# Gated linear recurrences in a hybrid block: chunk states replaced by scores of 128 and 256 tokens

## The chip, the cores and the metric

The kernel runs on one core of a Trainium2 chip. The metric is the device time of the program in microseconds (us). Engines are named as the profile names them: PE is TensorE (matmuls; PEld its weight loads), DVE is VectorE, ACT is ScalarE, POOL is GpSimd, SP is SyncE, whose queue issues most DMAs.

## The reference

The block normalises `x` (512 tokens of 2048 features), multiplies it by a wide input matrix, runs two token mixers in parallel, merges them with gates, projects and normalises. The change touches mixer A only, a gated linear recurrence with 8 heads of 128 features. The reference computes it in chunks of 64 tokens with a state between them:

```python
def step(state, inp):
    q_c, k_c, g_c, v_c = inp
    cum = jnp.cumsum(g_c, axis=1)
    inter = jnp.einsum('bthk,bhkv->bthv', q_c * jnp.exp(cum), state)
    diff = cum[:, :, None] - cum[:, None, :]
    decay = jnp.exp(jnp.where(causal[None, :, :, None, None], diff, -jnp.inf))
    scores = jnp.einsum('bthk,bshk,btshk->bhts', q_c, k_c, decay)
    intra = jnp.einsum('bhts,bshv->bthv', scores, v_c)
    last = cum[:, -1]
    new_state = (jnp.exp(last)[..., None] * state
                 + jnp.einsum('bshk,bshv->bhkv', k_c * jnp.exp(last[:, None] - cum), v_c))
    return new_state, inter + intra
```

Written without chunks, the output for token t is the sum over all s up to t of (q at t, times k at s, times the product of the forget gates f between them, summed over the 128 features) times v at s. `f` lies between 0 and 1, `k` is 1 - f. The output then goes through an RMS norm per head and a SiLU gate.

## The kernel before

**The order of the work.** The kernel is one long list of jobs, most of them projections: matmuls of the input matrix with the tokens, each as three float32r products of a high and a low half (`mm3`, lines 74 to 77). Side work is written as Python generators in lanes (line 180). After every few matmuls of a job `pump` (line 195) lets each lane take one step, up to the next `yield`. So the engines' queues hold a projection's matmuls, a step of each lane, the next matmuls, and so on, in the order in which the program issues them. `prep` (line 157) splits the next block of weights into halves, the high one on ACT (line 71), the low one on DVE (line 72), ahead of the matmuls that read them. The recurrences' lane comes first in a pump, ahead of the lane `top`, which selects keys for mixer B on DVE (lines 625 to 642). That lane takes iterations as far as a credit goes, and `R.load`, which the recurrences set before a yield, is the part of the credit that they claim for their own DVE work.

**One pair of heads.** `hgrn_gen(p)` (line 736) computes two heads (c is 0 or 1), and there are four pairs, in the order 3, 2, 0, 1. `q` and `k` are 128 features by 512 tokens for each head, plain float32, in one tile hqk, and all products of this generator use `mm` (line 79) on float32 operands.

- Levels 0 to 7 (lines 816 to 843) build the scores inside blocks of 128 tokens. At level l the tokens fall into halves of m = 2^(l-1); the products of the k of each earlier half with the q of the later half are the scores between the two. Then `decay(l)` (line 772) multiplies, on DVE, the q of the later halves by the total forget of the half before them and the k of the earlier halves by that of the half after them (`tot`), and the totals of two neighbouring halves are multiplied. After level 7, q and k carry the decay to the start and the end of their block of 128 tokens.
- The scores land in S (tile hS): 8 blocks of 128 by 128, four for each head. Small levels are gathered in `near` and copied (`nears`, line 812), levels 6 and 7 are copied by `spread_out` (line 804), all on ACT; S is filled with zeros on POOL beforehand (line 822).
- First step after the levels (lines 848 to 854): the k of blocks 0 to 2 are transposed on PE into a bank hkt (line 852) and copied to hkd (line 853).
- Second step (lines 857 to 870): three products per head, hkd with v, into a bank hp give what each block adds to the state (line 863); ACT copies the first, DVE forms the states of the second and third from the one before (line 867) in hst.
- Third step (lines 871 to 884): for each head seven products of 128 columns into a bank ho: v with the four blocks of S (line 878), and the states with the q of blocks 1 to 3 (line 880). ACT copies the result and its square (lines 881, 882).
- The rest is the norm (sums over features by a product with ones, into hz), the gate, and the split into halves hy that four DMAs write to DRAM (line 912). The tiles hz* and hy* take the places of hkd, hst, hq and hS (lines 886, 887, 909).

Of the kernel before, what the change touches and what calls it, by code (L numbers as in the profile page):

```python
# [26 lines left out]
F32 = mybir.dt.float32  # L27
FR = mybir.dt.float32r
AF = mybir.ActivationFunctionType
OP = mybir.AluOpType  # L30
# [4 lines left out]
T, D = 512, 2048  # L35
# [15 lines left out]
def hybrid_block(ctx, tc, x, w_in, w_uq, w_qidx, w_ukv, w_pa, w_pb, w_out, rel_bias, final_norm_w,  # L51
                 x_t, w_first, w_norm, w_cols, c_ident, c_levels, c_buckets, c_flip, out):
    nc = tc.nc
    V, A, G, PE, SP = nc.vector, nc.scalar, nc.gpsimd, nc.tensor, nc.sync
# [12 lines left out]
    def bank(name):  # L67
        return sdp.tile([128, 512], F32, name=name, tag="sd")
# [10 lines left out]
    def mm(ps, l, r, first, last):  # L79
        PE.matmul(ps, l, r, start=first, stop=last, skip_group_check=True)  # L80
# [35 lines left out]
    R = SimpleNamespace(load=0.0)  # L116
# [74 lines left out]
    def do_soon():  # L191
        while soon:
            soon.popleft()()
# [451 lines left out]
    def place(p, shape, dtype, name, tag):  # L645
        if p == 1 or tag not in ("hf", "hq"):
            return R.h.tile(shape, dtype, name=name, tag=tag)
        return R.i.tile(shape, dtype, name=name, tag=f"{tag}{p or 3}")
# [87 lines left out]
    def hgrn_gen(p):  # L736
        f, q = (hg[p, n] for n in "fq")
        gate = R.h.tile([128, 2, T], F32, name="hg")
        SP.dma_start(gate, gate_d[2 * p:2 * p + 2].rearrange("f p t -> p f t"))
        S = R.h.tile([128, 8, 128], F32, name="hS")  # L740
        near = R.h.tile([128, 8, 32], F32, name="hnear")
        G.memset(near, 0.0)
        qk = R.h.tile([128, 2, 2, T], F32, name="hqk")
# [3 lines left out]
        q0, tot = (a.rearrange("p c t -> p (c t)") for a in (q, f))  # L747
        q, k = qk[:, 0], qk[:, 1]
        qf, kf = (a.rearrange("p c t -> p (c t)") for a in (q, k))
# [4 lines left out]
        def scores(l, ps, qf=qf, kf=kf):  # L754

            m = 1 << l >> 1
            w = max(32, m)
            for n in range(8):
                for h in range(0, 128, w if l < 6 else 2 * w):
                    s = n * 128 + h  # L760
                    if l == 0:
                        o, r = ps[h:h + 32, n * 32:n * 32 + 32], q0[:, s:s + 32]
                    elif l < 6:
                        o = ps[h:h + 32, n * 16:n * 16 + 16]
                        r = qf[:, s:s + 32].rearrange("p (b a t) -> p a b t", a=2, t=m)[:, 1]
                    else:
                        g = h + m * (n % 2)
                        o = ps[g:g + m, n // 2 * m:n // 2 * m + m]
                        r = qf[:, s + m:s + 2 * m]
                    mm(o, kf[:, s:s + w], r, True, True)  # L770

        def decay(l):


            m = 1 << (l - 1)
            nb = 1024 // (2 * m)
            x = bass.AP(tensor=qf.tensor, offset=qf.offset + m, ap=[qf.ap[0], [1024 - m, 2], [2 * m, nb], [1, m]])
            tv = tot.rearrange("p (n a) -> p a n", a=2)
            V.tensor_tensor(x, x, tv[:, :, :, None].to_broadcast([128, 2, nb, m]), op=OP.mult)
            nt = R.h.tile([128, nb], F32, name=f"tot{l}", tag=f"tot{l % 2}")  # L780
            V.tensor_tensor(nt, tv[:, 0, :], tv[:, 1, :], op=OP.mult)
            return nt

        def take(l, ps):
            if l == 0:
                V.copy_predicated(near, R.levels[:, 0:1, :].to_broadcast([128, 8, 32]),
                                  ps[:, 0:256].rearrange("p (n t) -> p n t", n=8))
                return
            m = 1 << (l - 1)
            b = 16 // m  # L790
            mask = R.levels[:, l:l + 1, :].rearrange("p n (b a t) -> p n a b t", a=2, t=m)[:, :, 1]
            V.copy_predicated(near.rearrange("p n (b a t) -> p n a b t", a=2, t=m)[:, :, 1],
                              mask.to_broadcast([128, 8, b, m]),
                              ps[:, 0:128].rearrange("p (n b t) -> p n b t", n=8, t=m))

        def keep(l):

            m = 1 << (l - 1)
            nb = 1024 // (2 * m)
            x = bass.AP(tensor=qf.tensor, offset=qf.offset + m, ap=[qf.ap[0], [1024 - m, 2], [2 * m, nb], [1, m]])  # L800
            o = bass.AP(tensor=q0.tensor, offset=q0.offset + m, ap=[q0.ap[0], [-m, 2], [2 * m, nb], [1, m]])
            A.activation(o, x, AF.Copy)

        def spread_out(l, ps):
            m = 1 << (l - 1)
            for h in range(0, 128, 2 * m):
                for e in range(2):
                    g = h + m * e
                    A.activation(S[h:h + m, e::2, h + m:h + 2 * m],
                                 ps[g:g + m, 0:4 * m].rearrange("p (n t) -> p n t", n=4), AF.Copy)  # L810

        def nears(hs):
            for h in hs:
                A.activation(S[h:h + 32, :, h:h + 32], near[h:h + 32], AF.Copy)

        for l in range(1, 8):
            R.load = (0, 2.9, 1.6, 2.2, 1.5, 2.1, 1.4, 1.4)[l]
            if l % 2 == 0:
                do_soon()
                tot = decay(l)  # L820
                if l == 4:
                    G.memset(S, 0.0)
                if l == 6:
                    nears((0, 32))
                yield
                continue
            ps = bank("hl")
            at = 128 if l < 7 else 256
            if l == 1:
                scores(0, ps[:, 128:384])  # L830
            else:
                scores(l - 1, ps[:, at:at + 128], q0, q0)
            scores(l, ps)
            tot = decay(l)
            if l < 7:
                take(l - 1, ps[:, at:])
                take(l, ps)
                soon.append(lambda l=l: keep(l + 1))
            else:
                spread_out(6, ps[:, at:])  # L840
                spread_out(7, ps)
                nears((64, 96))
            yield

        R.load = 0.0
        if p == 1:
            yield
        kd = R.h.tile([128, 2, 3, 128], F32, name="hkd")
        for c in range(2):
            pt = bank("hkt")  # L850
            for j in range(3):
                PE.transpose(pt[:, j * 128:(j + 1) * 128], k[:, c, j * 128:(j + 1) * 128], R.ident)
            A.activation(kd[:, c], pt[:, :384].rearrange("p (j t) -> p j t", j=3), AF.Copy)
        yield
        while (p, "v") not in hg:
            yield
        R.load = 1.4
        v = hg[p, "v"]
        st = R.h.tile([128, 2, 3, 128], F32, name="hst")
        for c in range(2):  # L860
            pp = bank("hp")
            for j in range(3):
                mm(pp[:, j * 128:(j + 1) * 128], kd[:, c, j, :], v[:, j, c * 128:(c + 1) * 128],
                   j == 0, True)
            A.activation(st[:, c, 0, :], pp[:, 0:128], AF.Copy)
            for j in (1, 2):
                V.scalar_tensor_tensor(st[:, c, j, :], st[:, c, j - 1, :],
                                       tot[:, c * 4 + j:c * 4 + j + 1],
                                       pp[:, j * 128:(j + 1) * 128], op0=OP.mult, op1=OP.add)
        yield  # L870
        sq = k
        zs = []
        o = place(p, [128, 2, T], F32, "ho", "hf")
        for c in range(2):
            po = bank("ho")
            for j in range(4):
                sl = slice(j * 128, (j + 1) * 128)
                mm(po[:, sl], v[:, j, c * 128:(c + 1) * 128], S[:, 4 * c + j, :], j == 0, j == 0)
                if j:
                    mm(po[:, sl], st[:, c, j - 1, :], q[:, c, sl], False, True)  # L880
            A.activation(o[:, c], po, AF.Copy, scale=128 ** -0.5)
            A.activation(sq[:, c], po, AF.Square, scale=128 ** -0.5)
        R.load = 0.0
        yield
        for c in range(2):
            zs.append((place(p, [128, T], FR, "hzh", ("hkd", "hst")[c]),
                       place(p, [128, T], FR, "hzl", ("hq", "hS")[c])))
            split(*zs[c], sq[:, c])
        R.load = 1.4
        yield  # L890
# [2 lines left out]
        for c in range(2):  # L893
            ps = bank("hz")
# [10 lines left out]
        V.tensor_tensor(sq, sq, o, op=OP.mult)  # L905
        yield
        R.load = 1.3
        for c in range(2):
            y = [place(p, [128, T], FR, f"hy{i}", (("hkd", "hst"), ("hq", "hS"))[i][c]) for i in range(2)]
            split(*y, sq[:, c])  # L910
            for i in range(2):
                late[1].append(lambda y=y[i], i=i, h=2 * p + c: SP.dma_start(ya_d[i, h], y.bitcast(F32)))
# [713 lines left out]
```

## Time and profile before

| | |
|---|---|
| median of 3 runs | 1341.34 us (1340.42 to 1341.58) |
| the profiled execution | 1340.78 us |
| its span, first to last instruction | 1339.0 us |
| PE, DVE, ACT busy | 1328.2, 1067.2, 667.4 us |
| DVE combinations of states, line 867 | 16, each about 347 ns |
| ACT copies of transposes, line 853 | 8, each about 492 ns |
| ACT copies of 512 columns out of ho, line 881 | 8, each about 598 ns |

The profile is of one execution. Its page gives each engine's busy time and the chain of work that ended last. The views by tile list the instructions that write or read a tile (out<-in), with the least, median and largest duration in ns, their first and last start, and their shapes (partitions x elements). The chain in order of time and the timeline have a start in us, a length in us and an instruction (x4 means four merged into one line). A matmul's duration runs from its start to its modelled end, so neighbouring matmuls overlap; in the chain each has only the stretch that was its own. The view of waits says which engine and line waited for which, in total, how often, and at most. A row of the view of stretches has the stretch, its length, the busy time and count of PE, PEld, DVE, ACT and POOL, the granted clock of TensorE, the share of the DMA engines and GB/s.

### The profile page before, as it was taken

What the parts mean: (1) busy time and instruction counts of PE and PEld (TensorE: products, weight loads), DVE (VectorE), ACT (ScalarE), POOL (GpSimd) and SP (SyncE); (2) the same over time, 40 slices, a digit from 0 to 9 for tenths busy, and PEclk for the clock granted to TensorE, in tenths of its full rate; (3) what the DMA queues carried; (4) which work ended last, traced back from release to release, by engine and by line L of the source; (5) the groups of instructions that cost most, each with busy time, mean ns of one, the idle gap of its engine ahead of it and who ended that gap; (6) DMA issues with size and microseconds to landing.
All of it is one profiled execution on the core that took longest, in us unless ns stands there. A gap on an engine that the chain in (4) does not pass through costs nothing.

```text
span 1339.0 us, 26559 instructions
## 1 busy us (share of the span) xinstructions
PE 1328.2 (99%) x10876; PEld 1236.8 (92%) x10876; DVE 1067.2 (80%) x1705; ACT 667.4 (50%) x1060; POOL 35.7 (3%) x54
## 2 busy tenths in 40 slices
PE   9999999999999999999999999999999999999997
PEld 9988999999999999999999888888888888899996
DVE  7777889998888888886879989775656658899856
ACT  6455555454454444444666464656434423444435
POOL 2000000000000000000000000020001000000000
PEclk9999999999999999999999999999999999999999
DMA  6344545543454444434523525445755556653564
GB/s 242 95 114 113 151 142 158 154 138 104 142 158 143 142 142 142 135 107 164 182 84 103 182 72 159 125 151 176 242 191 191 186 177 218 202 161 124 163 208 164
DMA packets 141290, 205.82 MB, mean 154 GB/s; under 512 B 8672, under 2 KB 82032, under 8 KB 141040
## 3 DMA queue, kind: packets, MB, share of 16 engines
q1 hardware_dynamic: 140592, 203.78, 48.3%
q8 instruction: 85, 1.39, 0.4%
q10 hardware_dynamic: 576, 0.35, 0.1%
q14 instruction: 37, 0.30, 0.1%
HBM read 168.42 MB, written 35.68 MB: 152 GB/s over the span
## 4 chain that ended last, share of the span: by engine, by line
PE 95%; DVE 2%; ACT 1%; DMA 1%; issue 0%; SPq 0%; DVEq 0%; ACTq 0%
PE pp L75 15%; PE pp L77 15%; PE pp L76 15%; PE acc L75 14%; PE acc L77 14%; PE acc L76 14%; PE hl L80 1%; PE ho L80 1%; DMA xt<-in_x_t_dram 1%; PE sc L75 1%; PE sc L76 1%; PE sc L77 1%; PE hp L80 0%; PE po L77 0%; DVE xl L341 0%; PE po L76 0%
## 5 line engine op out<-in xcount | busy, mean ns | idle before, releaser
L150 ACT ACTIVATE bh<-wr 128x768 fp32r<-128x768 f32 x128 | 108.2, 845 | 215.5 <-issue 94.5
L152 ACT ACTIVATE wh<-sv 128x512 fp32r<-128x512 f32 x256 | 152.5, 623 | 84.3 <-DVE sv L145 66.6
L77 PE MATMUL pp<-sh,wl 128*128 128x256 f32 x624 | 172.7, 277 | 0.0
L75 PE MATMUL pp<-sh,wh 128*128 128x256 f32 x624 | 172.7, 277 | 0.0
L76 PE MATMUL pp<-sl,wh 128*128 128x256 f32 x624 | 172.6, 277 | 0.0
L72 DVE TENSOR_TENSOR wl<-wr,wh 128x1024 fp32r<-128x1024 f32 (+1 forms) x104 | 125.5, 1207 | 57.0 <-ACT wh L71 57.0
L154 DVE TENSOR_TENSOR wl<-sv,wh 128x1024 fp32r<-128x1024 f32 x128 | 156.4, 1222 | 5.8
L153 DVE TENSOR_TENSOR bl<-wr,bh 128x768 fp32r<-128x768 f32 x128 | 122.2, 955 | 47.2 <-ACT bh L150 46.9
L71 ACT ACTIVATE wh<-wr 128x1024 fp32r<-128x1024 f32 (+1 forms) x104 | 108.2, 1040 | 94.3 <-PE acc L76 40.6
L75 PE MATMUL acc<-xh,wh 128*128 128x512 f32 x304 | 120.3, 396 | 0.0
L77 PE MATMUL acc<-xh,wl 128*128 128x512 f32 x304 | 118.6, 390 | 0.0
L76 PE MATMUL acc<-xl,wh 128*128 128x512 f32 x304 | 118.5, 390 | 0.0
L76 PEld LDWEIGHTS pp<-sl,wh 128*128 128x128 f32 x624 | 117.3, 188 | 0.0
L77 PEld LDWEIGHTS pp<-sh,wl 128*128 128x128 f32 x624 | 117.3, 188 | 0.0
L75 PEld LDWEIGHTS pp<-sh,wh 128*128 128x128 f32 x624 | 117.3, 188 | 0.0
L75 PE MATMUL pp<-xh,bh 128*128 128x256 f32 x416 | 114.8, 276 | 0.0
L77 PE MATMUL pp<-xh,bl 128*128 128x256 f32 x416 | 114.8, 276 | 0.0
L76 PE MATMUL pp<-xl,bh 128*128 128x256 f32 x416 | 114.8, 276 | 0.0
L75 PE MATMUL acc<-yh,wh 128*128 128x512 f32 x256 | 100.3, 392 | 0.0
L76 PE MATMUL acc<-yl,wh 128*128 128x512 f32 x256 | 99.7, 390 | 0.0
L77 PE MATMUL acc<-yh,wl 128*128 128x512 f32 x256 | 99.7, 389 | 0.0
L145 DVE TENSOR_TENSOR sv<-wr 128x512 f32<-128x512 f32 x128 | 87.8, 686 | 8.2 <-DMA wr<-in_w_in_dram 5.1
(390 smaller groups left out, 3605.2 us busy)
## 6 DMA issues: line engine op xcount, KB each, us to landing
wr<-in_w_in_dram SPq DMA_DIRECT2D x136, 512.0 KB, 3.8
wr<-in_w_out_dram SPq DMA_DIRECT2D x32, 512.0 KB, 3.8
mg<-gate_d SPq DMA_DIRECT2D x48, 256.0 KB, 4.4
gate_d<-c SPq DMA_DIRECT2D x44, 256.0 KB, 4.7
wr<-in_w_in_dram SPq DMA_DIRECT2D x36, 256.0 KB, 3.0
wr<-in_w_pa_dram SPq DMA_DIRECT2D x16, 512.0 KB, 4.6
wr<-in_w_pb_dram SPq DMA_DIRECT2D x16, 512.0 KB, 4.1
wr<-in_w_qidx_dram SPq DMA_DIRECT2D x8, 512.0 KB, 4.0
```

Of the source, the lines that this page charges most:

```text
L71: A.activation(hi, src, AF.Copy)
L72: V.tensor_tensor(lo, src, hi.bitcast(F32), op=OP.subtract)
L75: PE.matmul(ps, lh, rh, start=first, stop=False, skip_group_check=True)
L76: PE.matmul(ps, lh, rl, start=False, stop=False, skip_group_check=True)
L77: PE.matmul(ps, ll, rh, start=False, stop=last, skip_group_check=True)
L80: PE.matmul(ps, l, r, start=first, stop=last, skip_group_check=True)
L145: V.tensor_tensor(sv[:, 0:2, :], b[:, 1:3, :], b[:, 0:1, :].to_broadcast([128, 2, 256]), op=OP.add)
L150: A.activation(bh, b[:, 1:4, :], AF.Copy)
L152: A.activation(vh[:, i:i + 2, :], sv[:, i:i + 2, :], AF.Copy)
L153: V.tensor_tensor(bl, b[:, 1:4, :], bh.bitcast(F32), op=OP.subtract)
L154: V.tensor_tensor(vl, sv, vh.bitcast(F32), op=OP.subtract)
```

## The change

States, transposes and `tot` as a multiplier of states go. In their place come two more levels of scores, between blocks of 128 tokens (level 8: blocks 0 and 1, blocks 2 and 3) and between halves of 256 tokens (level 9: blocks 0 and 1 with blocks 2 and 3), so that S holds the scores of every block with itself and every later block: ten blocks of 128 by 128 for each head in place of four. They lie in such an order that the scores of one block j with blocks j to 3 can be read at a constant step.

- First step: for each head two products of 128 columns, all four into one bank h8, and one copy on ACT into S; then one multiply on DVE over 512 elements (k of block 0 by the total of block 1, q of block 3 by the total of block 2, both heads), in place.
- Second step: for each head two products of 256 columns into a bank h9, and a copy on ACT.
- Third step: for each head four products, the v of block j with the whole row of scores, 512, 384, 256 and 128 columns wide, added up in the bank ho.
- S grows from 8 to 20 blocks, hkd and hst are gone, and the tiles of the norm and of the split take places in hS and hq. Only the four blocks on the diagonal of each head are filled with zeros.

```diff
-        S = R.h.tile([128, 8, 128], F32, name="hS")
+        S = R.h.tile([128, 20, 128], F32, name="hS")
+
+        def blocks(at, dims, s=S):
+            return bass.AP(tensor=s.tensor, offset=s.offset + at * 128, ap=[s.ap[0], *dims])
...
                 if l == 4:
-                    G.memset(S, 0.0)
+                    G.memset(blocks(3, [[1280, 2], [-128, 4], [1, 128]]), 0.0)
...
-        kd = R.h.tile([128, 2, 3, 128], F32, name="hkd")
+        ps = bank("h8")
         for c in range(2):
-            pt = bank("hkt")
-            for j in range(3):
-                PE.transpose(pt[:, j * 128:(j + 1) * 128], k[:, c, j * 128:(j + 1) * 128], R.ident)
-            A.activation(kd[:, c], pt[:, :384].rearrange("p (j t) -> p j t", j=3), AF.Copy)
+            for i in range(2):
+                s = slice(i * 256, i * 256 + 128)
+                mm(ps[:, (2 * c + i) * 128:(2 * c + i + 1) * 128], k[:, c, s],
+                   q[:, c, i * 256 + 128:i * 256 + 256], c == 0 and i == 0, True)
+        A.activation(blocks(5, [[1280, 2], [384, 2], [1, 128]]),
+                     ps.rearrange("p (c i t) -> p c i t", c=2, i=2), AF.Copy)
+        x = bass.AP(tensor=qf.tensor, offset=qf.offset + 384, ap=[qf.ap[0], [640, 2], [512, 2], [1, 128]])
+        tv = bass.AP(tensor=tot.tensor, offset=tot.offset + 2, ap=[tot.ap[0], [-1, 2], [4, 2], [0, 128]])
+        V.tensor_tensor(x, x, tv, op=OP.mult)
+        R.load = 0.7
+        yield
+        for c in range(2):
+            ps = bank("h9")
+            for i in range(2):
+                mm(ps[:, i * 256:i * 256 + 256], k[:, c, i * 128:i * 128 + 128], q[:, c, 256:512], i == 0, True)
+            A.activation(blocks(10 * c + 7, [[-384, 2], [256, 2], [1, 128]]),
+                         ps.rearrange("p (i n t) -> p i n t", i=2, n=2), AF.Copy)
+        R.load = 0.0
         yield
...
-        R.load = 1.4
         v = hg[p, "v"]
-        st = R.h.tile([128, 2, 3, 128], F32, name="hst")
-        for c in range(2):
-            pp = bank("hp")
-            for j in range(3):
-                mm(pp[:, j * 128:(j + 1) * 128], kd[:, c, j, :], v[:, j, c * 128:(c + 1) * 128],
-                   j == 0, True)
-            A.activation(st[:, c, 0, :], pp[:, 0:128], AF.Copy)
-            for j in (1, 2):
-                V.scalar_tensor_tensor(st[:, c, j, :], st[:, c, j - 1, :],
-                                       tot[:, c * 4 + j:c * 4 + j + 1],
-                                       pp[:, j * 128:(j + 1) * 128], op0=OP.mult, op1=OP.add)
-        yield
...
             for j in range(4):
-                sl = slice(j * 128, (j + 1) * 128)
-                mm(po[:, sl], v[:, j, c * 128:(c + 1) * 128], S[:, 4 * c + j, :], j == 0, j == 0)
-                if j:
-                    mm(po[:, sl], st[:, c, j - 1, :], q[:, c, sl], False, True)
+                n = (4, 3, 2, 1)[j]
+                mm(po[:, j * 128:], v[:, j, c * 128:(c + 1) * 128],
+                   blocks(10 * c + 3 - j, [[(256, 256, 896, 128)[j], n], [1, 128]]), j == 0, j == 3)
...
+        z = place(p, [128, 3, T], FR, "hzs", "hS")
+        zs = [(z[:, 0], place(p, [128, T], FR, "hzl", "hq")), (z[:, 1], z[:, 2])]
...
+        ys = place(p, [128, 3, T], FR, "hys", "hS")
```

The left-out lines adapt `spread_out` and `nears` to the new order of the blocks in S, with as many copies of the same sizes, and drop the tiles that z and y had.

More of the change, by code (lines that the diff above doesn't have):

```diff
@@ L808, in spread_out @@
                     g = h + m * e
-                    A.activation(S[h:h + m, e::2, h + m:h + 2 * m],
-                                 ps[g:g + m, 0:4 * m].rearrange("p (n t) -> p n t", n=4), AF.Copy)
+                    o = blocks(3 - e, [[1280, 2], [-256, 2], [1, m]], S[h:h + m, :, h + m:h + 2 * m])
+                    A.activation(o, ps[g:g + m, 0:4 * m].rearrange("p (c i t) -> p c i t", c=2, i=2), AF.Copy)
         def nears(hs):
             for h in hs:
-                A.activation(S[h:h + 32, :, h:h + 32], near[h:h + 32], AF.Copy)
+                o = blocks(3, [[1280, 2], [-128, 4], [1, 32]], S[h:h + 32, :, h:h + 32])
+                A.activation(o, near[h:h + 32].rearrange("p (c j) t -> p c j t", c=2), AF.Copy)
         for l in range(1, 8):
@@ L884, in hgrn_gen @@
         yield
+        z = place(p, [128, 3, T], FR, "hzs", "hS")
+        zs = [(z[:, 0], place(p, [128, T], FR, "hzl", "hq")), (z[:, 1], z[:, 2])]
         for c in range(2):
-            zs.append((place(p, [128, T], FR, "hzh", ("hkd", "hst")[c]),
-                       place(p, [128, T], FR, "hzl", ("hq", "hS")[c])))
             split(*zs[c], sq[:, c])
@@ L907, in hgrn_gen @@
         R.load = 1.3
+        ys = place(p, [128, 3, T], FR, "hys", "hS")
         for c in range(2):
-            y = [place(p, [128, T], FR, f"hy{i}", (("hkd", "hst"), ("hq", "hS"))[i][c]) for i in range(2)]
+            y = [ys[:, c], place(p, [128, T], FR, "hyl", "hq") if c == 0 else ys[:, 2]]
             split(*y, sq[:, c])
```

## The prediction

> **What bounds the kernel now.** I read the page first, then TensorE's waits and the stretches of time, then the matmuls of the part that changes, one tile at a time, with the chain of waits beside them.
>
> ```profile
> span 1339.0 us, 26559 instructions
> ...
> PE 1328.2 (99%) x10876; PEld 1236.8 (92%) x10876; DVE 1067.2 (80%) x1705; ACT 667.4 (50%) x1060; POOL 35.7 (3%) x54
> ...
> PE 95%; DVE 2%; ACT 1%; DMA 1%; issue 0%; SPq 0%; DVEq 0%; ACTq 0%
> ```
>
> TensorE is busy for 99% of the span and holds 95% of the chain that ended last. A busy TensorE need not be at its peak, since a matmul's recorded end is modelled, so I also look at what it waited for, and at the stretch in which the four pairs of recurrences run (from about 690 us to 925 us).
>
> ```profile
> engine line waited for: us in total, times, longest us
> PE acc L310 <- POOL ones_r L306: 1.4, 1, 1.4
> PE hl L80 <- DVE hqk L779: 0.7, 1, 0.7
> PE pf L80 <- POOL fh L336: 0.3, 1, 0.3
> PE pf L80 <- ACT xh L340: 0.3, 1, 0.3
> ```
> ```profile
> 690.00:925.00 235.00, 234.34 (x2969) 204.35 (x2968) 189.61 (x371) 133.19 (x211) 10.01 (x14) 1.00 0.43 131
> ```
>
> In those 235 us TensorE is busy for 234.34 (the first figure after the length), at the full clock (1.00). The one wait there is 0.7 us, for VectorE's decay before the last level. VectorE is busy 189.61 us and ScalarE 133.19 us, so both have room. Between the steps of a pair the projections' matmuls run, and they never starve. Hence the rule for this change: a microsecond of matmul added to these steps is a microsecond of the end, one taken away likewise, and VectorE's or ScalarE's work counts only where TensorE comes to wait for it.
>
> **What the steps cost now.** The rows of the tiles hkt (transposes), hp (chunk states), ho (values) and st (elsewhere, but the one plain float32 matmul that is 512 columns wide):
>
> ```profile
> L852 PE MATMUL hkt<-ident,hqk x24: 271/272/273, 721.0 to 896.7; 128*128 128x128 f32 x24
> ```
> ```profile
> L80 PE MATMUL hp<-hv,hkd x48: 271/275/275, 724.4 to 900.7; 128*128 128x128 f32 x48
> ```
> ```profile
> L80 PE MATMUL ho<-hS,hv x64: 270/275/275, 728.6 to 907.5; 128*128 128x128 f32 x64
> ...
> L80 PE MATMUL ho<-hqk,hst x48: 275/275/275, 729.0 to 907.7; 128*128 128x128 f32 x48
> ```
> ```profile
> L380 PE MATMUL st<-dg,ones_r x2: 590/590/591, 43.1 to 43.5; 128*128 128x512 f32 x2
> ```
>
> Counts first. A pair does 6 products into hp, so 24 over four pairs, and there are 48 records: a plain float32 matmul leaves two records. A transpose leaves one (6 by 4 is 24). The 275 ns are the time from a record's start to its modelled end and overlap with the next record; what a record costs is its share of the chain:
>
> ```profile
> 43.22 0.86 PE st L380 x2
> ...
> 737.77 0.93 PE hz L80 x4
> ```
> ```profile
> 721.17 0.66 PE hkt L852 x6
> 724.56 1.34 PE hp L80 x12
> 728.73 3.12 PE ho L80 x28
> ...
> 899.67 1.34 PE hp L80 x12
> ...
> 904.87 3.12 PE ho L80 x28
> ```
>
> So a record of 128 columns costs 1.34/12 or 3.12/28, 0.111 us each time, transposes too (0.66/6 is 0.110), and one of 512 columns costs 0.86/2, 0.43 us. That is 3.9 times the price for 4 times the columns: TensorE is paced by columns, and there is almost no fixed price per record. The line through the two points is 0.83 ns for a column and 0.005 us for a record, which gives 0.217 us at 256 columns and 0.324 at 384 (estimates between two measured ends).
>
> **The change on TensorE, for one pair.** Removed: the transposes (0.66), the chunk states (1.34) and the old values (3.12), together 5.12 us. Added:
> - Level 8, four products of 128 columns: 8 records by 0.111, 0.89 us.
> - Level 9, four products of 256 columns: 8 records by 0.217, 1.74 us.
> - Values, for each of the two heads one product each of 512, 384, 256 and 128 columns: of each width 4 records, 4 by (0.43 + 0.324 + 0.217 + 0.111), 4.33 us.
>
> The new sum is 6.96 us, 1.84 us more; over four pairs 7.4 us. There are fewer instructions (32 records for 46) but more columns: the two heads had 20 products of 128, 2560 columns, and now have 4096, while the six transposes saved were single records. The fourteen records saved are worth 14 times 0.005 us, which is in the sum already.
>
> These columns are what it costs to carry no state: the old form folds three chunks into states and reads one state for each later chunk; the new one multiplies every chunk's values by the scores of every chunk from there on.
>
> **The change on the other engines.** VectorE loses four combinations of 128 columns per pair (line 867) and gains one multiply of 512 elements, half of a decay. ScalarE loses two copies of 384 and two of 128 columns, and gains three of 512. All stand beside TensorE's work, with the projections' matmuls between the steps as cover (2.8 us from 721.58 to 724.40 in the rows below), and I count them at nothing, except for one wait. The filling of S with zeros covers as many elements as before. The number of yields is the same (three), so no queue is passed, SyncE's and GpSimd's included; the pool is as large as before (S grows by what the two dropped tiles held), and the y tiles go out by the same four DMAs; the zero fill of the next pair has to wait for the last of the four today already, since that one lies in S. The background selection on VectorE is told a load of 0.7 in one step in place of 1.4 in the next, which moves less than one of its iterations.
>
> **The added wait.** Level 9 needs the new multiply, which waits behind all that VectorE has queued, and the multiply waits for level 8, whose operands it overwrites. In its place stood hp, which waited only for ScalarE's copy of the transposes. How late VectorE would be is read from the step as it stands, in the first pair and in the third:
>
> ```profile
> 718.93 1.22 DVE L779 TENSOR_TENSOR hqk<-hqk,tot 128x1024 f32<-128x1024 f32 x1
> ...
> 723.69 1.23 DVE L72 TENSOR_TENSOR wl<-wr,wh 128x1024 fp32r<-128x1024 f32 x1 [1.03 <-ACT wh L71]
> 724.83 0.42 DVE L639 MAX8 m<-M 128x8 f32<-128x256 f32 x1
> ```
> ```profile
> 722.59 1.06 ACT L71 ACTIVATE wh<-wr 128x1024 fp32r<-128x1024 f32 x1
> 723.54 0.87 ACT L853 ACTIVATE hkd<-hkt 128x384 f32<-128x384 f32 x2
> ```
> ```profile
> 721.01 0.82 PE L852 MATMUL hkt<-ident,hqk 128*128 128x128 f32 x6
> 721.58 0.37 PE L75 MATMUL acc<-wh,xh 128*128 128x256 f32 x1
> ...
> 724.40 1.50 PE L80 MATMUL hp<-hv,hkd 128*128 128x128 f32 x12
> ```
> ```profile
> 840.01 1.23 DVE L72 TENSOR_TENSOR wl<-wr,wh 128x1024 fp32r<-128x1024 f32 x1 [1.17 <-ACT wh L71]
> 841.16 0.69 DVE L639 MAX8 m<-M 128x8 f32<-128x512 f32 x1
> ```
> ```profile
> 842.28 1.50 PE L80 MATMUL hp<-hv,hkd 128*128 128x128 f32 x12
> ```
>
> On ScalarE the copy of the transposes (line 853) comes behind the weight split wh, so that split is queued ahead of this step, and VectorE's half of it, wl, stands ahead of the new multiply. In the first pair wl ends at about 724.83 us. The multiply takes half of the decay's 1.22, 0.61 us, and is done at 725.44. TensorE would want level 9 at 724.40 plus 0.23 (level 8 is 0.89 where the transposes took 0.66), at 724.63: a stall of 0.8 us. While it waits, the projections behind it in order wait too, and nothing gives it back. In the third pair wl ends at 841.16, the multiply at 841.8, and level 9 is due at 842.5: room of 0.7 us. I take 0.8 us once. Its ends are nothing (if VectorE gets the multiply ahead of wl) and about 0.9 us in each pair, 3.6 us.
>
> **The sum.** 7.4 and 0.8 make 8.2 us. The profiled execution took 1340.78 us, so 1349.0 us; the median of the runs shown, 1341.34, is 0.56 above that execution.
>
> **Rivals.**
>
> *Wide records are cheap* (the other side: faster). If a record were paced by something other than its columns, by its weight load or its issue, wide rows would win. The place is level 9 and the values. The price: the float32r record of 512 columns (hz above) costs 0.93/4, 0.23 us, and if plain float32 cost no more at that width, with 0.174 and 0.116 at 384 and 256, level 9 would be 0.93 us and the values 2.53; with level 8 that is 4.35 us, 0.77 less than today, 3.1 us less over four pairs, 1337.7 us. It decides from the point where a 512-column record costs under about 0.29 us (there 0.89, level 9 and the values add up to 5.12 again). The row against it is st: 0.43.
>
> The Trainium skill, "TensorE: Matmul & The Clock Gate", section "Back-to-back issue gap", says for sustained streams that a matmul of 128 columns takes about 81 ns and one of 512 about 131. By that ratio of 1.62 a 512-column record would be 0.18 us here, and the kernel some 3.3 us faster (an estimate from that page). This trace disagrees, with its ratio of 3.9.
>
> *No change.* The added columns fill gaps that TensorE has, or the shorter work of VectorE gives time back. The gap in the stretch is 0.7 us in all, and it lies before level 7, ahead of anything that changes. At most 1341 us, and only if the steps' matmuls do not delay what follows, against 234.34 busy of 235.
>
> *More waits.* The multiply is late in all four pairs, or ScalarE's copies of the levels come late for the values: 7.4 and up to 3.6 us, about 1351.8. For it: the first pair is late by its rows. Against it: the third pair has room, and seven levels with the same pattern of decay and product cost one wait of 0.7 us in four pairs.
>
> **How the numbers follow.** 0.82 for the forecast, 0.11 for more waits, 0.04 for no change, 0.03 for cheap wide records. A measurement of this kernel can tell about 0.2%, 2.7 us, from no change; the first two cases are slower by more than that. So faster 0.03, same 0.04, slower 0.93. For the range: without the stall the time is 1348.1, from which I take the 0.7 us wait, should the shift of the steps remove it, and 1.2 us, by which the runs shown differ (1340.42 to 1341.58): 1346.2. The top is more waits, 1351.8, with 0.7 us for the runs: 1352.5.
>
> **What would show it.** Right: hkt and hp are gone; the chain has 8 records of level 8 in about 0.89 us, 8 of level 9 in about 1.74, and 16 of the values in about 4.33 per pair; TensorE's busy time and the span both grow by some 8 us; its waits gain one row of about 0.8 us, for VectorE's new multiply. Wrong: 16 value records in under 3 us (columns are not the price), a TensorE that waits in every pair for the multiply or for a copy, or a stretch from level 1 of the first pair to the end of the last that is not longer than today.

## The result, and the profile after

The changed kernel took 1350.13 us (median of 4 runs, 1349.23 to 1350.79), the kernel before 1340.92 us beside it (4 runs). The ratio is 1.0066, with a 95% interval of 1.0053 to 1.0079: slower by 9.2 us, where 8.2 were forecast; the time lies 1.1 us above the forecast of 1349.0 and inside its range of 1346.2 to 1352.5. A second set of runs of the same kernel gave 1349.34 us against 1341.17, 8.2 us more (ratio 1.0062, 1.0049 to 1.0075). The profiled execution of the changed kernel took 1350.32 us.

The page after, the lines that answer to those of before:

```profile
span 1348.5 us, 26429 instructions
...
PE 1337.3 (99%) x10820; PEld 1238.8 (92%) x10820; DVE 1065.9 (79%) x1693; ACT 668.3 (50%) x1056; POOL 38.5 (3%) x54
...
PE 96%; DVE 2%; ACT 1%; DMA 0%; issue 0%; POOL 0%; SPq 0%; ACTq 0%
```

TensorE is still busy for 99%, and its busy time grew by 9.1 us with 56 fewer records: the span (9.5 us more) follows TensorE, not the count of instructions. Not all of the 9.1 us is the change: the products account for 7.2, as the chain below shows, and about 1.0 is a later start, which the next section takes up. What TensorE waited for, after:

```profile
PE acc L310 <- POOL ones_r L306: 1.4, 1, 1.4
PE h L80 <- DVE hqk L863: 0.7, 1, 0.7
PE pf L80 <- POOL fh L336: 0.6, 1, 0.6
PE hl L80 <- DVE hqk L783: 0.3, 1, 0.3
```

There is one new row: level 9 (the trace calls both new banks h) waits 0.7 us, once, for the new multiply on VectorE (line 863). The other row on the recurrences was there before, at line 779. The chain after, first the first pair, then the second:

```profile
726.32 1.99 PE h L80 x8
731.05 4.31 PE ho L80 x16
...
784.84 0.89 PE h L80 x8
788.49 1.73 PE h L80 x8
792.97 4.31 PE ho L80 x16
```

Level 8 took 0.89 us, level 9 1.73 us and the values 4.31 us in the second pair, as in the third and fourth. That is 6.93 us where 5.12 stood: 1.81 us more for a pair. In the first pair, where the wait stands in front of it, level 9 took 1.99 us, 0.26 more; I call this the restart. The traces do not show what it consists of. VectorE in that pair, and below it ScalarE:

```profile
724.43 1.22 DVE L72 TENSOR_TENSOR wl<-wr,wh 128x1024 fp32r<-128x1024 f32 x1 [1.01 <-ACT wh L71]
725.58 0.68 DVE L863 TENSOR_TENSOR hqk<-hqk,tot 128x512 f32<-128x512 f32 x1
```
```profile
723.34 1.06 ACT L71 ACTIVATE wh<-wr 128x1024 fp32r<-128x1024 f32 x1
724.29 0.60 ACT L859 ACTIVATE hS<-h 128x512 f32<-128x512 f32 x1
```

The multiply stands right behind the low half of the weights, which itself waited 1.01 us for the high half on ScalarE. Level 9 starts at 726.32, as soon as the multiply is through; the timeline puts the wait at 0.75 us.

### The profile page after: what moved, and what is told of

Its sections match the earlier page's. It is cut to its first block, busy times and chain, and to the rows that moved or that the text cites. A ratio compares the mean times of both kernels' runs of the same rounds, so it can differ in the third digit from the quotient of the medians.

```text
span 1348.5 us, 26429 instructions
## 1 busy us (share of the span) xinstructions
PE 1337.3 (99%) x10820; PEld 1238.8 (92%) x10820; DVE 1065.9 (79%) x1693; ACT 668.3 (50%) x1056; POOL 38.5 (3%) x54
## 4 chain that ended last, share of the span: by engine, by line
PE 96%; DVE 2%; ACT 1%; DMA 0%; issue 0%; POOL 0%; SPq 0%; ACTq 0%
PE pp L77 15%; PE pp L75 15%; PE pp L76 15%; PE acc L75 13%; PE acc L77 13%; PE acc L76 13%; PE pf L80 2%; PE ho L80 1%; PE hl L80 1%; PE h L80 1%; PE sc L75 1%; PE sc L76 1%; PE sc L77 1%; PE po L77 0%; DVE hqk L783 0%; PE po L76 0%
```

## Experiments

The runs came in three sets, each on a chip of its own with the kernel before beside it; that kernel's medians were 1341.17, 1341.00 and 1341.26 us. The theory: TensorE is paced by columns, and one wait comes on top. The rivals are that records and not columns are what costs, that the new chain of product, multiply and copy costs by itself, and that part of the gap is not the change at all.

**The same kernel again**, no edit:

> The changed kernel itself, beside the next three on one chip. Theory (TensorE is paced by columns: some 1.8 us more per pair, and one wait of level 9 for VectorE's multiply in the first pair, worth about 1.0 us with the restart): some 1350.1 us, ratio to the kernel before 1.0066 within 0.0008; one wait of about 0.7 us at the multiply. Rival (part of the 9.2 us is not the steps but the start, which began 0.7 us later in the profiled execution): the first product of the recurrences starts at the same time as in the kernel before, and the ratio is nearer to 1.0060.

1349.34 us. The wait of 0.7 us is there. The rival is right about the profiled executions: the first product of the recurrences began at 694.85 us before, at 695.82 in the first profile after and at 696.02 in this one, though nothing differs ahead of it; in a profile further down (the doubled copies) the same kernel up to there began at 694.95. So up to 1.2 us between two profiled executions is their start, and of the 9.5 us by which the span grew about 1.0 is. How much of it is in the medians (9.2 and 8.2 us more) is not shown, since the other executions left no trace. A measure without the start is the time from the first product of the recurrences to the norm of the last pair (tile hz): 222.35 us before, 230.93 and 231.21 in the two profiles of the changed kernel, 8.6 and 8.9 more.

**Level 9 twice:**

```diff
             for i in range(2):
                 mm(ps[:, i * 256:i * 256 + 256], k[:, c, i * 128:i * 128 + 128], q[:, c, 256:512], i == 0, True)
+            for i in range(2):
+                mm(ps[:, i * 256:i * 256 + 256], k[:, c, i * 128:i * 128 + 128], q[:, c, 256:512], i == 0, True)
```

> The products of level 9 are issued twice into the same bank, which changes nothing in the result. Theory (a microsecond of matmul in these steps is a microsecond of the end): 8 more records of 256 columns per pair by 0.216 us, 1.73 us, over four pairs 6.9 us more than the changed kernel, about 1357.0 us. Rival (part of the added columns falls into time that TensorE has anyway): less than 5 us more.

1356.53 us (ratio 1.0113, 1.0100 to 1.0127), 7.2 us above the changed kernel in the same set. Its chain in the second pair:

```profile
785.78 0.89 PE h L80 x8
789.43 3.45 PE h L80 x16
795.64 4.31 PE ho L80 x16
```

Sixteen records in 3.45 us where eight took 1.73: 1.72 us a pair, 6.9 in all, and all of it arrives at the end. There is no gap on TensorE into which products could fall.

**Values cut into pieces of 128 columns:**

```diff
-                n = (4, 3, 2, 1)[j]
-                mm(po[:, j * 128:], v[:, j, c * 128:(c + 1) * 128],
-                   blocks(10 * c + 3 - j, [[(256, 256, 896, 128)[j], n], [1, 128]]), j == 0, j == 3)
+                for t in range(j, 4):
+                    at = 10 * c + 3 - j + (2, 2, 7, 1)[j] * (t - j)
+                    mm(po[:, t * 128:t * 128 + 128], v[:, j, c * 128:(c + 1) * 128],
+                       S[:, at, :], j == 0 and t == 0, t == j)
```

> The changed kernel with every value product cut into pieces of 128 columns: 40 records per pair in place of 16, the same columns. Theory (columns pay, a record costs about 0.005 us of its own): 24 records by 0.005 is 0.12 us per pair, 0.5 us in all, about 1350.6 us. Rival (a wide record is cheap because it saves a weight load or an issue, so that the wide rows are worth something in themselves): with 0.05 us for a record 1.2 us per pair, 4.8 us more, about 1355 us.

1349.93 us (ratio 1.0068, 1.0055 to 1.0081), the time of the changed kernel. The values in the second pair, 40 records in place of 16:

```profile
792.57 4.46 PE ho L80 x40
```

0.15 us for 24 more records, 0.006 us each. That the values meet whole rows is worth 0.6 us over the four pairs and no more; a record's own price is next to nothing.

**The copies on ScalarE twice:** line 859 and line 870 each get a second, identical copy behind them.

> Each of the three new copies on ScalarE is issued twice (12 more copies of 512 columns, 0.6 us each, 7.2 us of ScalarE). Theory (ScalarE's work is beside TensorE's): nothing, within 0.5 us of the changed kernel. Rival (the copies of the levels come late for the values, or hold up the weights behind them): 0.6 us or more per pair, 2.4 us more.

1349.64 us (ratio 1.0068, 1.0054 to 1.0082), no change. ScalarE was busy 675.1 us in place of 668.3, and none of it is on the path.

**The multiply on GpSimd:**

```diff
-        V.tensor_tensor(x, x, tv, op=OP.mult)
-        R.load = 0.7
+        G.tensor_tensor(x, x, tv, op=OP.mult)
+        R.load = 0.0
```

> The new multiply goes to GpSimd, so it no longer stands behind the low half of the weights on VectorE. Theory (the wait in the first pair is VectorE's queue): TensorE's wait there goes, 0.7 to 1.0 us less than the changed kernel, about 1349.2 us; the products keep their prices. Rival (the chain level 8, multiply, level 9 is itself too long for one step): the wait stays or grows, and with a slower engine it appears in the other pairs as well, 1351 us or more.

The load that the step claims on VectorE goes to 0 with it. 1350.56 us (ratio 1.0071, 1.0057 to 1.0085), 1.2 us above the changed kernel in the same set: no gain. But the two theories come apart in the trace. Its waits, then GpSimd in the fourth pair, then the first pair's level 9 in the chain:

```profile
PE h L80 <- POOL hqk L863: 1.4, 1, 1.4
```
```profile
904.00 0.46 POOL L972 TENSOR_TENSOR MB<-M,bh 128x128 f32<-128x128 f32 x1 [18.11 <-DMA bh<-bh_d]
904.41 2.11 POOL L975 TENSOR_TENSOR MB<-M,bh 128x256 f32<-128x256 f32 x3
906.48 1.05 POOL L863 TENSOR_TENSOR hqk<-hqk,tot 128x512 f32<-128x512 f32 x1
```
```profile
725.17 1.73 PE h L80 x8
```

In the first pair the wait is gone (level 9 takes 1.73 us again), so it was VectorE's queue. In the fourth pair the multiply now stands behind mixer B's bias sums, which wait for a DMA, and TensorE waits 1.4 us there. The queue was changed for another one, with its own work in front, and the multiply itself took 1.05 us in place of 0.68.

**The multiply on GpSimd in the first pair only:** `(G if p == 3 else V).tensor_tensor(x, x, tv, op=OP.mult)`.

> The multiply goes to GpSimd in the first pair only, where nothing is queued on it; in the other pairs it stays on VectorE. Theory: the wait of 0.7 us and the restart behind it, 1.0 us together, go and nothing takes their place: 1348.5 to 1349.3 us, 0.8 to 1.0 less than the changed kernel, and no row of TensorE waiting for the multiply. Rival (the stretch is short of ScalarE or VectorE anyway, so that the next product waits instead): no gain, 1349.8 or more, with a wait in another row of the first pair.

1348.74 us (ratio 1.0058, 1.0045 to 1.0070), inside what was expected, and the waits have no row of the multiply left. What remains above the kernel before, 7.5 us, is the columns' 7.2 to within what such a comparison can tell. From the first product of the recurrences to the norm of the last pair this profile has 229.75 us: 7.4 more than the kernel before, and 1.2 less than the changed kernel.

**One state between the halves, in four steps.** Level 8 stays; two transposes, two products and one product of the state with 256 columns of q for each head take the place of level 9:

```diff
-                mm(ps[:, i * 256:i * 256 + 256], k[:, c, i * 128:i * 128 + 128], q[:, c, 256:512], i == 0, True)
+                PE.transpose(pt[:, j * 128:(j + 1) * 128], k[:, c, j * 128:(j + 1) * 128], R.ident)
...
         v = hg[p, "v"]
+        for c in range(2):
+            pp = bank("hp")
+            for j in range(2):
+                mm(pp[:, 0:128], S[:, 10 * c + 4 + 3 * j, :], v[:, j, c * 128:(c + 1) * 128], j == 0, j == 1)
+            A.activation(S[:, 10 * c + 6, :], pp[:, 0:128], AF.Copy)
+        yield
...
-                n = (4, 3, 2, 1)[j]
+                n = (2, 1, 2, 1)[j]
...
+            mm(po[:, 256:512], S[:, 10 * c + 6, :], q[:, c, 256:512], False, True)
```

> Level 8 stays, level 9 goes: one state per head carries blocks 0 and 1 to blocks 2 and 3 (two transposes after the multiply, two products added up in the bank, one product of the state with 256 columns of q), in one more step. Theory by columns, per pair: level 8 0.89, four transposes 0.44, states 8 records by 0.111 or 0.89, values 4 records each of 256, 128, 256 and 128 columns and 4 of 256 with the state, 3.49; together 5.71, which is 0.59 more than before and 1.25 less than the changed kernel. Over four pairs 2.4 us above the kernel before, and the wait of the first pair again (the transposes need the multiply), up to 1.0: 1343.3 to 1344.4 us. Rival (what costs is the new chain of steps and copies, not the columns): the chain of level 8, multiply and wait is kept and one more step and copy are added, so as slow as the changed kernel, 1349 us or more.

1354.47 us (ratio 1.0096, 1.0082 to 1.0109): the theory as I had put it failed by 10 us, although the products cost what it says (0.89, 0.44, 0.89 and 3.48 us in the chain). The waits name another place:

```profile
PE acc L75 <- ACT gs L1205: 3.0, 1, 3.0
PE hz L80 <- ACT hzs L71: 1.7, 1, 1.7
```

Neither is in the steps that changed. The second is a product of the norm right behind the split it reads; the first is the projection after the last gates' job. Both stand where the list of jobs empties the recurrences' lane before it goes on (the jobs `open_att` and `end_hgrn`). A pair that has a step left there runs it with nothing between. The added step, not the state, would then be at fault. The next three tell this apart.

**The changed kernel with one empty step more**, a second `yield` between the multiply and level 9:

> One more yield between the multiply and level 9, so that a whole stretch of projection matmuls lies between them and the multiply has twice the time. Theory (the wait in the first pair is VectorE's queue): the wait of 0.7 us goes, 0.7 to 1.0 us less than the changed kernel, about 1349.2 us. Rival (VectorE is late there by more than a step, or the last pairs end later because of the added step): no gain, or more.

1358.56 us (ratio 1.0132, 1.0118 to 1.0146), 8.4 and 9.2 us above the changed kernel's two medians for a step that holds nothing. The wait of the first pair is gone, as the theory said; the two waits just shown came in its place, 3.0 and 1.7 us, and the waits before the levels grew from 0.3 us to 1.9 in all.

**The kernel before with one empty step more**, a second `yield` after the transposes (line 854):

> The kernel before with one more empty yield in each pair, after the transposes. It adds no work. Theory (a pair has no step to spare: with one more, the last steps of the third and the fourth pair run back to back at the points where the lane is drained, and TensorE waits there for ScalarE): 6 to 9 us above the kernel before, with TensorE waiting at hz for the copy in front of it and at the projection after the gates' job for ScalarE, and no waits elsewhere. Rival (only the changed kernel's steps are that tight, since they are longer): within 1 us of the kernel before.

1350.93 us (ratio 1.0070, 1.0056 to 1.0084; the five runs lie between 1349.04 and 1351.54), 9.7 us more, a little above the range; 8.5 us in the profiled execution (span 1347.5). Its waits, and TensorE's clock around and after the second of them, which ends at 860.81 (the third figure from the end):

```profile
PE acc L75 <- ACT gs L1194: 3.0, 1, 3.0
PE hz L80 <- ACT hzh L71: 1.7, 1, 1.7
```
```profile
855.00:860.00 5.00, 4.12 (x33) 3.78 (x31) 0.00 (x0) 2.99 (x6) 0.00 (x0) 1.00 0.00 0
860.00:864.00 4.00, 2.97 (x7) 2.16 (x8) 2.62 (x4) 3.94 (x7) 0.00 (x0) 0.67 0.00 0
864.00:868.00 4.00, 4.00 (x18) 3.24 (x17) 2.27 (x3) 2.71 (x4) 0.00 (x0) 0.90 0.05 19
```

So the kernel before is as tight as the changed one, and the penalty belongs to the schedule. Of its 8.5 us these two waits and one of 0.2 for VectorE at hz hold 4.9, the levels 0.5, a later start 0.4, and the clock's fall some 1.2 (six records at 0.43 us in place of 0.23). The last 1.5 us lie in TensorE's busy time, which grew by 2.7 us (from 1328.2 to 1330.9) where the clock explains 1.2; what they are stays open.

**One state between the halves, in three steps.** The transposes move into the first step and read k before the multiply, which then covers q alone; VectorE joins the two blocks:

```diff
...
+            A.activation(S[:, 10 * c + 6, :], pp[:, 0:128], AF.Copy)
+            V.scalar_tensor_tensor(S[:, 10 * c + 6, :], S[:, 10 * c + 6, :], tot[:, c * 4 + 1:c * 4 + 2],
+                                   pp[:, 128:256], op0=OP.mult, op1=OP.add)
+        R.load = 0.7
+        yield
...
```

> The columns of the kernel with one state between the halves, but in three steps: the transposes are taken in the first step from the k before the multiply (which then covers q of block 3 alone), and VectorE joins the two blocks into the state. Theory (columns set the cost; the kernel with four steps lost the rest because its last steps fell behind the fixed points where the lane is drained): level 8 0.89, transposes 0.44, states 0.89, values 3.49, 5.71 us per pair against 5.12 before, 2.4 us over four pairs, and no wait of the second step for VectorE: 1343.4 us, ratio 1.0018. Rival (the chain of level 8, multiply and copies costs by itself, whatever the columns): 1349 us or more, as slow as the kernel with four steps or the changed kernel.

1343.86 us (11 runs; ratio 1.0020, 1.0011 to 1.0028), 2.6 us more than the kernel before where 2.4 were expected. The second pair in the chain:

```profile
782.27 0.89 PE h L80 x8
783.16 0.44 PE hkt L864 x4
...
786.36 0.89 PE hp L80 x8
790.01 3.48 PE ho L80 x20
```

5.70 us of products, 0.58 above the kernel before, a third of the way to the changed kernel; its only wait in the recurrences is the 0.7 us before level 7. From the first product of the recurrences to the norm of the last pair it took 224.79 us, 2.4 more than before, where four times 0.58 are 2.3. So the chain of level 8, copies and state costs nothing beyond its columns. The multiply's wait is not tested here, since it covers q alone and only the values, two steps later, need it. With the same columns in four steps the kernel took some 10 us more.

## Why the prediction was right

**The bound.** TensorE paces this stretch: 6.9 us of doubled products arrived in full, 6.8 us of added copies on ScalarE did not arrive at all.

**The price of a record.** The line through two measured widths, 0.217 us at 256 columns and 0.324 at 384, was the step on which the sum stood. Level 9 was forecast at 1.74 us and took 1.73, the values at 4.33 and took 4.31. Four pairs by 1.81 are 7.2 us, forecast 7.4. Cutting the rows and taking one state in place of level 9 (three steps) moved the time as columns say.

**The rival of cheap wide records** is out: 24 records more cost 0.15 us a pair. The Trainium skill's figures in "TensorE: Matmul & The Clock Gate", section "Back-to-back issue gap" (81 ns at 128 columns, 131 at 512), do not hold for these products: by that ratio the 16 records of the four widths would have taken about 2.3 us (an estimate from that page), and they took 4.31.

**The added wait** was forecast at 0.8 us, in the first pair alone. The wait was 0.75 us, and with the restart of 0.26 us it cost 1.0; the restart is what the forecast left out. With GpSimd in that pair the trace shows it gone, and the stretch from the first product to the last norm is 1.2 us shorter (229.75 against 230.93): 1.0 for the wait and its restart, and 0.2 in the levels of the fourth pair, which come up below. The medians, 0.6 and 1.4 us under those of the changed kernel, are of the right size but too coarse to show it. The columns came out a little under their term and the wait a little over it, which partly cancels in the sum. The third pair had the room that its rows showed.

**The work counted at nothing** was nothing on ScalarE, as the doubled copies showed. Under "The change on the other engines" I wrote that the number of yields is the same, so no queue is passed. That was true, and worth more than the sentence gave it: one step more would have cost as much as the whole change, on either kernel. The forecast named no price for it, and the expectation for one state in four steps went wrong by just that.

**What was not forecast:** the start of a profiled execution varies by up to 1.2 us, and some 0.2 us came in among the levels of the fourth pair (its first level stood 7.48 us later than before, 874.47 against 866.99, and a later one 7.70, 890.43 against 882.73). Before, then after, VectorE's decay between the two:

```profile
872.99 1.25 DVE L779 TENSOR_TENSOR hqk<-hqk,tot 128x1024 f32<-128x1024 f32 x1 [0.35 <-ACT hq L802]
```
```profile
880.44 1.72 DVE L783 TENSOR_TENSOR hqk<-hqk,tot 128x1024 f32<-128x1024 f32 x1 [0.33 <-ACT hq L806]
882.21 0.74 PE L80 MATMUL hl<-hqk 128*32 128x16 f32 x64
```

The products that read k begin when this decay ends, and it took 1.72 us in place of 1.25. In the second profile of the changed kernel it took 1.80, and the same stretch of levels was 0.3 us longer than before; with level 9 doubled it took 1.32, and the stretch was as before (15.74 us). Why the decay is sometimes slower is not shown.

No version tried beats the kernel before, and of the three forms its states are the shortest by columns (5.12, 5.70 and 6.93 us a pair).

## What to carry to other kernels

Where the matmul engine has no gaps, count its columns before its instructions: fewer and wider products of plain float32 gain almost nothing per column (0.15 us in 4.3 here), and a recurrence that folds the past into a state saves columns against scores of everything with everything. Before adding a wait, look at what the awaited engine has queued in front at that moment; moving the work to another engine changes which queue that is, and helped here in the first pair, where GpSimd's queue was empty. In a schedule of steps with fixed points at which lanes are emptied, count the steps too.

## What the runs showed of the hardware

In the kernel before with one empty step more, TensorE's granted clock was 0.67 in the 4 us around the end of a wait of 1.7 us and the one of 0.2 us behind it (0.43 us for a float32r record of 512 columns, then 0.23 again); after the wait of 3.0 us in the same execution the clock stayed at 1.00. In the changed kernel with one empty step more, which has the same waits, it was the other way round: full clock after the first, and 0.57 after the one of 3.0 us:

```profile
945.00:949.00 4.00, 0.96 (x9) 0.72 (x8) 3.50 (x3) 3.21 (x5) 2.42 (x3) 1.00 0.70 262
949.00:953.00 4.00, 4.00 (x11) 3.13 (x12) 2.12 (x4) 3.47 (x7) 0.00 (x0) 0.57 0.76 236
```
With one state in four steps, which has the same waits again, the clock fell after both (0.70 from 864 to 868 us, 0.57 from 944 to 948). The Trainium skill, "TensorE: Matmul & The Clock Gate", section "Part 1: The HAM clock gate", puts the fall to half speed after at least one idle window of about 3.4 us on a counter that runs freely. Like waits that end differently agree with a counter that runs freely, though no run here shows the counter; that 3.4 us of idleness are needed does not agree, since waits of 1.9 us in all were enough here.

A plain float32 product leaves two records (64 of level 8 and 9 for 32 products). In a stream of them a record costs 0.11 us at 128 columns, 0.22 at 256 (1.73 us for eight) and 0.43 at 512: 0.83 ns for a column and about 0.005 us of its own. A transpose of 128 by 128 is one record at the same 0.11 us.
